# First modulation in four parts, and a last MLP group that gates W2 and adds onto x in the bank

## The chip, the cores and the metric

The kernel runs on one core of a Trainium2 chip. The metric is device microseconds of one execution. Engines are TensorE (PE; its weight loads are listed as PEld), VectorE (DVE), ScalarE (ACT), GpSimd (POOL) and SyncE (SP), which issues the transfers. All five run beside each other, each in the order of its own instruction stream, and wait for one another by semaphores.

## The reference, cut to what matters

Two layers work on 640 tokens, five tiles of 128 (tile 0 is context, tiles 1 to 4 are latents), with D_MODEL = 1024 and D_FF = 4096. Each sub-layer is

```
x <- LayerNorm(ALPHA * x + gate * f(x * (1 + scale) + shift)),   eps 1e-5
(shift, scale, gate) = columns of SiLU(cond) @ w_mod[l] + b_mod   (cond: c for latents, c_ctx for context)
layer 0: f = [retention | differential attention] @ w_out,  heads from one product with w_in
layer 1: f = [windowed attention | gated linear attention] @ w_out
MLP:     f(h) = square(relu(h @ w_1)) @ w_2
lambda of the differential attention = exp(sum(p0*p1)) - exp(sum(p2*p3)) + lam_init
```

Outputs are x of both groups, and keys, values and states of the context. The first step of all is shift and scale of layer 0, on which everything else depends; the last is the sum over D_FF in W2, the gate, the addition to x and a LayerNorm with its own g and b.

## The kernel before, in words

Every fp32 operand of a product is split into a high and a low part (fp32r), and a product becomes three: hi x hi, hi x lo, lo x hi. A weight comes in units of 128x1024 (512 KB): SP loads it into one of NRAW = 3 buffers `wraw`, ACT casts it to `whi`, and DVE subtracts to get `wlo` (`Unit.split`, line 525). A raw buffer is free again when `wlo` is made. Activations are kept in the same way (`h0h`, `h0l`; `ghi`, `glo` in the MLP).

The order of all instructions on PE, ACT, DVE and POOL is written into the program: a planner (`Order`) lets generators of work take turns by a time that it keeps for each engine, and what it has issued stays in that order. SP's order comes from the framework's scheduler; at most eight transfers are in flight, since each waits for the one eight before it. In the start, up to `start.close()`, the order is the one in which the code stands.

**The start** (lines 1000 to 1128) computes shift and scale of layer 0 in two halves of four feature tiles each. `load_mod0(h, k)` loads two tiles 128x512 of weights, `matvec` multiplies them by the SiLU of the conditioning vectors into a bank `mod0` (profile name `mod`; 32x256 products at line 468), `mod_row` copies it (ACT, `mrow`), `mod_cols` transposes it on PE (`modT`, line 483) and adds the bias on DVE (`first_mod`, `sc`), and `modulated` applies it to one token tile (ACT and POOL, `h`; then DVE's `h0h`, `h0l`). `early_part(t, h)` are the first products of layer 0's input projection for that half, into banks `early`; tiles 2 and 3 share a double bank. EARLY gives the step k of the second half's `matvec` ahead of which a tile's products stand; TURN is the order of tiles for the last half. `lam(dls)` computes the lambda above from `diff_lam`, whose load (`dl`) is issued after the first half's `xT` tiles.

**The end** is group g = 7 of eight in the last layer's MLP. Each group adds four blocks of 128 rows of W2. For the earlier groups the product is collected in `y`; in the last one, for each tile t and each half of the columns, `mlp_block` (line 1994) runs 12 products into a bank `fps`, DVE multiplies it by the gate row (`tmp`) and adds it to x. Then `norm` (line 929) takes statistics on DVE (`bn`, `mv`, `r`, `nmr`), ACT normalises, and POOL multiplies by g and adds b (`lnrow`), both 128x512; the last tile does all but its first quarter on DVE. SP sends x out in 11 transfers.

Line 379 is the helper through which all instructions of ACT, DVE and POOL go, 468 is a product, 483 a transpose, 452 a transfer. In the profile the digits of names are left out: `wmod` is also `w_mod0`'s tile, `sc` is `sc1`, `h` is `h32`.

Of the kernel before, what the change touches and what calls it, by code (L numbers as in the profile page):

```python
# [406 lines left out]
def trunk_kernel(ctx: ExitStack, tc: tile.TileContext, io: dict, layers: int = 2, stop: str = ""):  # L407
# [105 lines left out]
    class Unit:  # L513


        def __init__(self, src, kt, n, own=False):
            self.src, self.kt, self.n, self.own = src, kt, n, own
# [143 lines left out]
    done = set()  # L661
    pieces = {}
# [19 lines left out]
    for l in range(layers):  # L682
# [246 lines left out]
    def norm(t, rows, ft, A, B, final, key, xd=None):  # L929
# [4 lines left out]
        for i, (a, c0, c1) in enumerate(cuts):  # L934
            dve.bn_stats(st[:, i, :], X[t][a][:, c0:c1])
# [14 lines left out]
        if final:  # L950

            cut = (1024, 1024, 1024, 1024, 256)[t]
            for a, c0, c1 in ((0, 0, 256), (0, 256, 512), (1, 0, 512)) if t == NT - 1 else ((0, 0, 512), (1, 0, 512)):
                c, far = slice(c0, c1), 512 * a + c1 <= cut
                x, g, b = X[t][a][:, c], rows[0][a][:, c], rows[1][a][:, c]
# [7 lines left out]
                load(io["y"][t * P:(t + 1) * P, 512 * a + c.start:512 * a + c.stop], x)  # L963
            return
# [35 lines left out]
    def load_mod0(h, k):  # L1000
        raws[h, k] = [slot("wmod0"), slot("wmod0")]
        for a in range(2):
            load(raws[h, k][a][:, :512], io["w_mod0"][h, k, :, 512 * a:512 * a + 512])

    def matvec(h, k, ps):
        raw = raws.pop((h, k))
        for j in range(4):
            mm(ps[32 * j:32 * j + 32, :256], cs[:, k, :], raw[j // 2][:, 256 * (j % 2):256 * (j % 2) + 256],
               start=(k == 0), stop=(k == KT - 1))

    def load_x(h):
        xt = [slot("xT") for _ in range(4)]
        for k in range(4):
            load(xt[k][:, :TOK], io["xT"][4 * h + k])
        return xt

    def mod_row(ps):
        row = slot("mrow")
        act.copy(row[:, :256], ps[:, :256])
        return row  # L1020

    def mod_cols(h, row):
        tp = acc("modT")
        for e in range(2):
            transpose(tp[:, tcol(e)], row[:, tcol(e)])
        for s in range(2):
            o = V_BM + 8 * s + 4 * h
            vec_tt(first_mod[:, s, 4 * h:4 * h + 4, :].rearrange("p (b e) r -> p e b r", e=2),
                   tp[:, :256].rearrange("p (e s b r) -> p e s b r", e=2, s=2, b=2)[:, :, s, :, 0:2],
                   vec[:, o:o + 4].rearrange("p (b e) -> p e b", e=2).unsqueeze(3).broadcast_to([P, 2, 2, 2]), op=ALU.add)  # L1030
        dve.tensor_scalar(sc1[:, 4 * h:4 * h + 4, :], first_mod[:, 1, 4 * h:4 * h + 4, :], 1.0, None, op0=ALU.add)

    def modulated(h, xt, t):
        r_ = 1 if t == 0 else 0
        h32 = slot("h32")
        for b in range(4):
            k = 4 * h + b
# [5 lines left out]
        h4 = h32[:, :512].rearrange("p (b c) -> p b c", b=4)  # L1043
        hi = ft.h[h][:, :, tcol(t)]
        dve.tensor_copy(hi, h4)
        vec_tt(ft.l[h][:, :, tcol(t)], h4, hi.bitcast(F32), op=ALU.subtract)
# [7 lines left out]
    def early_part(t, h):  # L1054
        for n in range(2):
            w, o, c = pieces[0, EVEN[n]], early_bank(t)[:, 256 * n:256 * n + 256], tcol(t)
            for k in range(4 * h, 4 * h + 4):
# [9 lines left out]
    def lam(dls):  # L1067
# [16 lines left out]
    load_unit()  # L1084
    xt = load_x(0)
    load_unit()
    load_unit()
    ps = acc("mod0")
    for k in range(KT):
        matvec(0, k, ps)  # L1090
    row = mod_row(ps)
    split_unit()
    load_unit()
# [3 lines left out]
    for k in range(KT):  # L1097
        load_mod0(1, k)
    xt1 = load_x(1)
    load(cst[:, C_RC:], io["consts"][:, C_RC:])  # L1100
    mod_cols(0, row)
    order.give()
    warm(early_bank(0)[:, :128], 14)
    modulated(0, xt, 0)
    split_unit()
    for t in range(1, NT):
        modulated(0, xt, t)
    split_unit()
    split_unit()
    lam(dls)  # L1110
    ps = acc("mod0")
    for k in range(KT):
        for t in range(NT):
            if EARLY[t] == k:
                early_part(t, 0)
        matvec(1, k, ps)
    row = mod_row(ps)
    early_part(3, 0)
    mod_cols(1, row)
    order.give()  # L1120
    early_part(4, 0)
    load_unit()
    for t in TURN:
        modulated(1, xt1, t)
# [162 lines left out]
    def even_mixer(ft, cat, out_half):  # L1287
# [221 lines left out]
        for t in TURN:  # L1509
            split_hold[0] = t in TURN[:2]  # L1510

            def step():
                pos[1] = 2
                early_part(t, 1)
# [411 lines left out]
    def layer(l, ft, xd):  # L1926
# [34 lines left out]
        for g in range(8):  # L1961
# [14 lines left out]
            else:  # L1976
                if g == 6:
                    need_mods(l, (5,))
                    rows = gate_rows(l, 1)
                for f in range(4):  # L1980
# [13 lines left out]
            def mlp_block(t, nh):  # L1994
                w = use((l, "2", g, nh), (l, "2", g, 0) if last else None)
# [149 lines left out]
```

## Time and profile before

| | |
|---|---|
| median of three runs | 1635.65 us (1634.84 to 1637.54) |
| the profiled execution | 1635.63 us, of it the span 1633.8 us |
| TensorE busy | 1570.0 us, 96% |
| DVE, ACT, POOL busy | 62%, 37%, 32% |
| mean granted TensorE clock | 0.993 |
| chain that ended last, by engine | PE 80%, DVE 6%, ACT 5%, POOL 4%, DMA 2% |
| transfers | 177.75 MB, 109 GB/s over the span |

An engine's busy time is a sum over the whole span. The change is at its two ends, so the lines to read are those of the first 65 us and of the last 45 us. A line of a timeline gives start, duration, engine, program line, operation, result and operand, and in brackets how long the engine was idle before it and what it waited for; like instructions that follow each other are put together (x4), and their duration is then that of the whole stretch.

### The profile page before, as it was taken

Reading aid. Unit: us, or ns where it says so; the run is one execution under the profiler, and the core shown is the slowest. Engines: PE = TensorE matmul, PEld = TensorE weight load, DVE = VectorE, ACT = ScalarE, POOL = GpSimd, SP = SyncE. Lnnn points to the kernel's source line nnn. Section 1 sums busy time; section 2 is a strip of 40 time slices with the busy share of each in tenths; the row PEclk is TensorE's granted clock in tenths of the full one; section 3 lists DMA queues with packets and bytes.
Section 4 is the critical chain, followed back from the end, with each engine's and each line's share of the span. In section 5 each row is a group of like instructions: output and inputs, shape, how many; then the busy total and the mean of one; then the engine's idle time right before and its main releaser. Section 6 shows DMA issues by size and latency. Waiting matters only on the chain.

```text
span 1633.8 us, 28517 instructions
## 1 busy us (share of the span) xinstructions
PE 1570.0 (96%) x11345; PEld 1421.7 (87%) x11345; DVE 1018.0 (62%) x1943; ACT 610.4 (37%) x1279; POOL 524.7 (32%) x451
## 2 busy tenths in 40 slices
PE   7999999999999999999999998889999999999996
PEld 4998999999889889988988887779989988998994
DVE  3776662676477677676786788777824444444457
ACT  2554443336323222222255555553633222322321
POOL 2110000012467777777537347231200010011226
PEclk9999999999999999999999999999999999999998
DMA  9633334341444444463324101114212222223121
GB/s 333 204 119 118 102 98 162 130 134 52 139 136 143 148 139 152 147 182 114 112 68 139 61 28 39 56 43 155 79 52 78 78 78 72 71 75 113 58 78 65
DMA packets 89844, 177.75 MB, mean 109 GB/s; under 512 B 23648, under 2 KB 30832, under 8 KB 89712
## 3 DMA queue, kind: packets, MB, share of 16 engines
q1 hardware_dynamic: 89712, 175.94, 33.6%
q8 instruction: 89, 1.46, 0.4%
q14 instruction: 43, 0.35, 0.1%
HBM read 169.40 MB, written 6.50 MB: 108 GB/s over the span
## 4 chain that ended last, share of the span: by engine, by line
PE 80%; DVE 6%; ACT 5%; POOL 4%; DMA 2%; issue 2%; SPq 0%; POOLq 0%; DVEq 0%; ACTq 0%
PE ff L468 25%; PE fps L468 24%; PE proj L468 11%; PE ops L468 6%; PE fproj L468 3%; ACT h L379 1%; PE early L468 1%; DMA wmod<-in_w_mod 1%; POOL x L379 1%; PE sd L468 1%; PE po L468 1%; DVE wlo L379 1%; POOL y L379 1%; PE odp L468 1%; PE gl L468 1%
## 5 line engine op out<-in xcount | busy, mean ns | idle before, releaser
L468 PE MATMUL ff<-hh,whi 128*128 128x320 f32 (+2 forms) x960 | 297.2, 310 | 0.0
L468 PE MATMUL ff<-hh,wlo 128*128 128x320 f32 (+2 forms) x960 | 296.5, 309 | 0.1
L468 PE MATMUL ff<-hl,whi 128*128 128x320 f32 (+2 forms) x960 | 296.4, 309 | 0.0
L379 ACT CAST whi<-wraw 128x1024 fp32r<-128x1024 f32 (+1 forms) x183 | 189.3, 1045 | 285.4 <-PE fps L468 250.5
L379 DVE TENSOR_TENSOR wlo<-wraw,whi 128x1024 fp32r<-128x1024 f32 (+1 forms) x183 | 244.2, 1339 | 68.8 <-ACT whi L379 68.6
L468 PE MATMUL fps<-wlo,ghi 128*128 128x512 f32 (+1 forms) x648 | 253.9, 392 | 2.0 <-DVE wlo L379 2.0
L468 PE MATMUL fps<-whi,ghi 128*128 128x512 f32 (+1 forms) x648 | 254.5, 393 | 0.0
L468 PE MATMUL fps<-whi,glo 128*128 128x512 f32 (+1 forms) x648 | 253.5, 391 | 0.0
L379 POOL TENSOR_TENSOR x<-x,lnrow 128x512 f32<-128x512 f32 (+1 forms) x78 | 110.4, 1429 | 347.9 <-DVE y L379 216.7
L468 PEld LDWEIGHTS ff<-hh,whi 128*128 128x128 f32 x960 | 180.2, 188 | 3.1 <-issue 2.1
L379 DVE TENSOR_TENSOR relu<-relu 128x320 f32<-128x320 f32 (+3 forms) x100 | 64.1, 641 | 189.5 <-ACT ghi L379 185.9
L468 PEld LDWEIGHTS ff<-hl,whi 128*128 128x128 f32 x960 | 180.2, 188 | 0.6
L468 PEld LDWEIGHTS ff<-hh,wlo 128*128 128x128 f32 x960 | 180.2, 188 | 0.4 <-DVE wlo L379 0.4
L379 ACT ACTIVATE relu<-ff 128x320 f32<-128x320 f32 (+3 forms) x100 | 51.4, 514 | 295.2 <-PE ff L468 295.2
L379 DVE TENSOR_TENSOR y<-fps,y 128x512 f32<-128x512 f32 x120 | 82.6, 689 | 117.8 <-PE fps L468 117.7
L468 PEld LDWEIGHTS fps<-wlo,ghi 128*128 128x128 f32 x648 | 121.8, 188 | 29.9 <-DVE wlo L379 2.9
L468 PEld LDWEIGHTS fps<-whi,ghi 128*128 128x128 f32 x648 | 121.6, 188 | 29.6 <-issue 2.5
L468 PEld LDWEIGHTS fps<-whi,glo 128*128 128x128 f32 x648 | 121.7, 188 | 28.0
L379 POOL TENSOR_SCALAR wmod<-wmod,cs 128x512 f32<-128x512 f32 x84 | 95.2, 1134 | 124.1 <-DVE moda L379 108.5
L379 POOL TENSOR_TENSOR moda<-moda,wmod 128x512 f32<-128x512 f32 x84 | 123.5, 1470 | 6.2
L468 PE MATMUL ops<-wlo,cath 128*128 128x256 f32 x320 | 90.2, 282 | 2.2 <-DVE wlo L379 2.2
L468 PE MATMUL proj<-whi,hh 128*128 128x256 f32 (+1 forms) x280 | 83.9, 300 | 8.6 <-DVE sg L379 5.7
(295 smaller groups left out, 3372.2 us busy)
## 6 DMA issues: line engine op xcount, KB each, us to landing
wraw<-in_w SPq DMA_DIRECT2D x128, 512.0 KB
wmod<-in_w_mod SPq DMA_DIRECT2D x128, 256.0 KB
wmodp<-in_w_mod SPq DMA_DIRECT2D x64, 256.0 KB
wraw<-in_w_even SPq DMA_DIRECT2D x24, 512.0 KB
wraw<-in_w_out SPq DMA_DIRECT2D x16, 512.0 KB
wraw<-in_w_odd SPq DMA_DIRECT2D x16, 512.0 KB
gate<-mrow SPq DMA_DIRECT2D x16, 256.0 KB
xT<-in_xT SPq DMA_DIRECT2D x8, 320.0 KB
```

Source lines behind the costliest of these rows:

```text
L379: i = f(*a, **k)
L468: nc.tensor.matmul(o, a, b, **kw)
```

## The change

1. The first modulation is done in four quarters of two feature tiles: `w_mod0` comes as [4, 8, 128, 512], one transfer for each step k, `matvec` has 32x128 products, `load_x` loads two tiles at a time, `modulated` does two feature tiles. The start is one loop over the quarters. In it the load of `dl`, with those of `sink` and the constants, stands behind the last quarter's `xT`, and `lam(dls)` stands in the second quarter's turn.
2. For the latent tiles the last group's four units of W2 are loaded once more as `("gated", n)`; POOL multiplies them by the gate's columns before they are split. Tile 0 uses the ungated units.
3. For the latent tiles ACT copies x into the bank (tile `out`) behind a dummy product that starts the bank; the block's products add onto it. DVE's product with the gate and its addition to x are gone; `norm` reads the banks.
4. In the final `norm` the second half of tiles 1 to 3 goes to DVE, in two passes, where it was on ACT and POOL; the last tile has four parts of 256 columns, and there are 12 output transfers.

```diff
@@ Unit.split
+            if self.gate is not None:
+                for k in range(self.kt):
+                    c = slice(k * self.n, (k + 1) * self.n)
+                    pool.tensor_tensor(raw[:, c], raw[:, c], last_gates[self.gate][:, :self.n], op=ALU.mult)
@@ order of the weights, behind the last layer's pieces
+    for n in range(2):
+        add_piece(("gated", n), [Unit(io["w_2"][layers - 1, 7, n, u], 2, 512, gate=n) for u in range(2)])
@@ norm: source() gives the bank where there is one, else X[t][a]
-            dve.bn_stats(st[:, i, :], X[t][a][:, c0:c1])
+            dve.bn_stats(st[:, i, :], source(a, c0, c1))
...
-            cut = (1024, 1024, 1024, 1024, 256)[t]
+            cut = (1024, 512, 512, 512, 256)[t]
...
                 if far:
-                    act.activation(x, x, AF.Identity, scale=r, bias=nmr)
+                    act.activation(x, y, AF.Identity, scale=r, bias=nmr)
...
                 else:
-                    stt(x, x, mv[:, 0:1], g, op0=ALU.subtract, op1=ALU.mult)
+                    stt(x, y, mv[:, 0:1], g, op0=ALU.subtract, op1=ALU.mult)
@@ start
+    for q in range(3):
+        for k in range(KT):
+            load_mod0(q, k)
+        if q == 0:
+            load_unit()
+        xts.append(load_x(q))
...
     for k in range(KT):
-        load_mod0(0, k)
...
+        load_mod0(3, k)
+    xts.append(load_x(3))
     dls = slot("dl")
     bc_row(dls[:, :256], io["diff_lam"])
     bc_row(sk, io["swa_sink"])
-    for k in range(KT):
-        load_mod0(1, k)
-    xt1 = load_x(1)
     load(cst[:, C_RC:], io["consts"][:, C_RC:])
...
+    for q in range(4):
         for t in range(NT):
+            if q or t:
+                modulated(q, xts[q], TURN[t] if q == 3 else t)
+        if q == 3:
+            break
+        if q == 1:
+            split_unit()
+            split_unit()
+            load_unit()
+            lam(dls)
+        ps = acc("mod0")
+        for k in range(KT):
+            for t in range(NT):
+                if EARLY[t] == k:
+                    early_part(t, q)
+            matvec(q + 1, k, ps)
+        row = mod_row(ps)
+        early_part(3, q)
+        mod_cols(q + 1, row)
+        order.give()
+        early_part(4, q)
@@ last group of the last layer
+                def preload():
+                    if todo:
+                        t, a, c0, c1 = todo.pop(0)
+                        ps = (acc if t in (1, 3) or c0 else pss)("out", True)
+                        banks.setdefault(t, {})[a, c0, c1] = ps
+
+                        hv = parts[0][0]
+                        mm(ps[:, :c1 - c0], hv[:, :128], hv[:, :c1 - c0], start=True, stop=False)
+                        act.copy(ps[:, :c1 - c0], X[t][a][:, c0:c1])
+
+                def whole_block(t, a, c0, c1):
+                    preload()
+                    w = use(("gated", a), ("gated", 0))
+                    c, n, ps = tcol(t), slice(c0, c1), banks[t][a, c0, c1][:, :c1 - c0]
+                    for f in range(4):
+                        hv, lv = parts[f]
+                        mm(ps, hv[:, c], w.hi(f, n), start=False, stop=False)
+                        mm(ps, hv[:, c], w.lo(f, n), start=False, stop=False)
+                        mm(ps, lv[:, c], w.hi(f, n), start=False, stop=(f == 3))
...
+                        for b in blocks:
+                            if b[0] == t:
+                                order.gemm(lambda: whole_block(*b))
```

**Where the instructions stand.** SP's order in the start, in before: the load of `dl` (`diff_lam`) stands ahead of the second half's weights `wmod0`.

```order
L452 DMA rd_522<-in_ret_decay 128x8
L452 DMA wmod_967_5452<-in_w_mod 128x512
L452 DMA wmod_968_5454<-in_w_mod 128x512
L452 DMA dl_36_202<-in_diff_lam 128x256
L452 DMA wmod0_37_205<-in_w_mod0 128x512
L452 DMA wmod0_38_206<-in_w_mod0 128x512
```

SP's order in the changed kernel, where the load of `dl` is row 53:

```order
L452 DMA wmod0_56_262<-in_w_mod0 128x512
L452 DMA wmod0_57_264<-in_w_mod0 128x512
L452 DMA xT_58_266<-in_xT 128x640
L452 DMA xT_59_267<-in_xT 128x640
L452 DMA dl_60_270<-in_diff_lam 128x256
L452 DMA wraw_77_427<-in_w_even 128x1024
```

The load moved behind all 32 tiles `wmod0` and all eight `xT`. DVE's order in the changed kernel around the use of `dl`; `first_mod` here is that of the third quarter:

```order
L379 TENSOR_TENSOR wlo_76_424<-wraw_39_228,whi_75_423 128x1024
L379 TENSOR_TENSOR dl_60_270<-dl_60_270 128x128
L379 TENSOR_REDUCE ls_109<-dl_60_270 128x2
L379 TENSOR_TENSOR nlam_110<-ls_109 128x1
L379 TENSOR_SCALAR nlam_110<-nlam_110 128x1
L379 TENSOR_SCALAR nsink_112<-sink_111 128x8
L379 TENSOR_TENSOR first_mod_100<-modT_80_518,vec_87 128x4 x2
L379 TENSOR_SCALAR sc1_101<-first_mod_100 128x4
L379 CAST h0h_2_103<-h32_81_535 128x2x128
```

In before the same rows stand in the same order, with the second half's `first_mod` behind them. POOL's order at the end of the program in before; `y` belongs to the groups ahead, `x` to the final products of tiles 0 and 1:

```order
L379 TENSOR_TENSOR y_2376_14079<-y_2376_14079,gate_2667_16313 128x512
L379 TENSOR_TENSOR x_2162_12786<-x_2162_12786,lnrow_2746_17011 128x512
L379 TENSOR_TENSOR x_2201_13014<-x_2201_13014,lnrow_2747_17013 128x512
L379 TENSOR_TENSOR x_2162_12786<-x_2162_12786,lnrow_2748_17015 128x512
L379 TENSOR_TENSOR x_2201_13014<-x_2201_13014,lnrow_2749_17017 128x512
L379 TENSOR_TENSOR x_2168_12831<-x_2168_12831,lnrow_2746_17011 128x512
```

The same place in the changed kernel; `wraw` are the four units of W2 that POOL gates, each in two halves:

```order
L379 TENSOR_TENSOR y_2392_14187<-y_2392_14187,gate_2683_16421 128x512
L379 TENSOR_TENSOR wraw_2758_17059<-wraw_2758_17059,gate_2682_16419 128x512 x2
L379 TENSOR_TENSOR wraw_2761_17091<-wraw_2761_17091,gate_2682_16419 128x512 x2
L379 TENSOR_TENSOR wraw_2787_17186<-wraw_2787_17186,gate_2683_16421 128x512 x2
L379 TENSOR_TENSOR x_2178_12894<-x_2178_12894,lnrow_2764_17123 128x512
L379 TENSOR_TENSOR x_2217_13122<-x_2217_13122,lnrow_2765_17125 128x512
L379 TENSOR_TENSOR x_2178_12894<-x_2178_12894,lnrow_2766_17127 128x512
L379 TENSOR_TENSOR x_2217_13122<-x_2217_13122,lnrow_2767_17129 128x512
L379 TENSOR_TENSOR wraw_2800_17239<-wraw_2800_17239,gate_2683_16421 128x512 x2
L379 TENSOR_TENSOR x_2184_12939<-x_2184_12939,lnrow_2764_17123 128x512
```

Three units stand ahead of tile 0's four final products, the fourth behind them. ACT's order at that place in the changed kernel; `whi` are the casts of the units, `out` the copies of x into banks, `x` the final activations of tile 0:

```order
L379 CAST whi_2780_17157<-wraw_2748_16960 128x1024
L379 COPY out_2782_17161<-x_2184_12939 128x512
L379 COPY out_2788_17188<-x_2222_13156 128x512
L379 CAST whi_2785_17182<-wraw_2758_17059 128x1024
L379 CAST whi_2789_17193<-wraw_2761_17091 128x1024
L379 COPY out_2801_17241<-x_2194_12987 128x512
L379 ACTIVATE sq_2794_17215<-mv_2792_17210,eps_t_90 128x1
L379 ACTIVATE x_2178_12894<-x_2178_12894,nmr_2797_17218,r_2796_17217 128x512
L379 ACTIVATE x_2217_13122<-x_2217_13122,nmr_2797_17218,r_2796_17217 128x512
L379 CAST whi_2798_17235<-wraw_2787_17186 128x1024
L379 CAST whi_2802_17246<-wraw_2800_17239 128x1024
```

The casts of the gated units come behind copies of x, and those of the third and fourth unit behind the final activations of tile 0.

## Rows read from the trace of the kernel before

**Rows 1.** Page, part 1: busy us, share, instructions.

```profile
PE 1570.0 (96%) x11345; PEld 1421.7 (87%) x11345; DVE 1018.0 (62%) x1943; ACT 610.4 (37%) x1279; POOL 524.7 (32%) x451
```

**Rows 2.** Chain of waits, first 62 us: start us, duration us, what.

```profile
36.62 0.62 PE mod L468 x4
...
44.78 0.22 PE modT L483 x2
44.99 17.09 PE early L468 x144
```

**Rows 3.** Windows: us, busy PE PEld DVE ACT POOL, PE clock, DMA share, GB/s.

```profile
0.00:9.00 9.00, 2.63 (x12) 0.59 (x12) 0.92 (x6) 1.50 (x2) 0.20 (x4) 1.00 0.75 230
9.00:18.00 9.00, 8.29 (x52) 2.09 (x52) 0.00 (x0) 0.17 (x1) 0.00 (x0) 1.00 0.97 336
18.00:27.00 9.00, 7.17 (x54) 6.40 (x54) 5.48 (x11) 6.04 (x13) 5.56 (x7) 1.00 1.04 392
27.00:36.00 9.00, 7.10 (x59) 4.08 (x60) 5.07 (x7) 2.21 (x3) 2.53 (x4) 1.00 0.97 340
36.00:47.00 11.00, 10.95 (x101) 9.16 (x102) 1.94 (x10) 2.06 (x6) 1.36 (x3) 1.00 1.04 400
```

**Rows 4.** Timeline of DVE, ACT and POOL, 36 to 53 us.

```profile
36.14 0.28 DVE L379 TENSOR_TENSOR dl<-dl 128x128 f32<-128x128 f32 x1
36.46 0.29 DVE L379 TENSOR_REDUCE ls<-dl 128x2 f32<-128x128 f32 x1
...
36.78 0.20 ACT L379 ACTIVATE ls<-ls 128x2 f32<-128x2 f32 x1 [1.81 <-DVE ls L379]
41.79 0.37 ACT L379 COPY mrow<-mod 128x256 f32<-128x256 f32 x1 [4.80 <-PE mod L468]
...
45.03 0.24 DVE L379 TENSOR_TENSOR first_mod<-modT,vec 128x8 f32<-128x8 f32 x2 [7.59 <-PE modT L483]
...
45.64 7.14 POOL L379 TENSOR_SCALAR h<-xT,sc,first_mod 128x128 f32<-128x128 f32 x10 [16.11 <-DVE sc L379]
...
46.56 0.43 DVE L379 CAST h0h<-h 128x512 fp32r<-128x512 f32 x1 [1.08 <-POOL h L379]
```

**Rows 5.** Timeline of PE: a later modulation's 32x128 products.

```profile
64.86 1.08 PE L468 MATMUL modp<-wmodp,cs 128*32 128x128 f32 x32
```

**Rows 6.** Windows around a gap of TensorE, columns as in Rows 3.

```profile
1056.00:1058.00 2.00, 0.00 (x0) 0.00 (x0) 1.76 (x10) 1.91 (x6) 0.00 (x0) 0.66 0.76 279
1058.00:1060.00 2.00, 0.73 (x3) 0.76 (x4) 1.36 (x7) 1.64 (x6) 1.22 (x2) 0.50 0.01 2
1060.00:1062.00 2.00, 2.00 (x12) 2.00 (x11) 0.00 (x0) 2.00 (x7) 1.65 (x2) 0.50 0.00 0
1062.00:1064.00 2.00, 2.00 (x13) 2.00 (x12) 0.48 (x2) 1.07 (x3) 1.63 (x3) 0.63 0.00 0
```

**Rows 7.** Chain of waits, last 49 us: the last group's first products.

```profile
1589.73 2.81 PE fps L468 x12
```

**Rows 8.** Timelines of ACT, DVE, POOL and PE, last 46 us.

```profile
1590.67 1.04 ACT L379 CAST whi<-wraw 128x1024 fp32r<-128x1024 f32 x1
...
1593.90 1.22 DVE L379 TENSOR_TENSOR wlo<-wraw,whi 128x1024 fp32r<-128x1024 f32 x1
...
1604.95 0.69 DVE L379 TENSOR_TENSOR tmp<-fps,gate 128x512 f32<-128x512 f32 x1
...
1621.13 0.41 DVE L379 BATCH_NORM_STATS2 bn<-x 128x6 f32<-128x256 f32 x1
...
1622.98 0.74 DVE L379 SCALAR_TENSOR_TENSOR x<-x,mv,lnrow 128x256 f32<-128x256 f32 x1
...
1605.21 5.97 POOL L379 TENSOR_TENSOR x<-x,lnrow 128x512 f32<-128x512 f32 x4 [38.45 <-ACT x L379]
1611.63 19.43 POOL L379 TENSOR_TENSOR x<-x,lnrow 128x512 f32<-128x512 f32 x14 [0.46 <-ACT x L379]
...
1618.55 0.28 PE L468 MATMUL fps<-whi,glo 128*128 128x256 f32 x1
```

More of the change, by code (lines that the diff above doesn't have):

```diff
@@ L513, in trunk_kernel, with __init__ @@
     class Unit:
-        def __init__(self, src, kt, n, own=False):
-            self.src, self.kt, self.n, self.own = src, kt, n, own
+        def __init__(self, src, kt, n, own=False, gate=None):
+            self.src, self.kt, self.n, self.own, self.gate = src, kt, n, own, gate
         def load(self):
@@ L927, in summed, with norm, source @@
             stt(x, x, ALPHA, y, op0=ALU.mult, op1=ALU.add)
-    def norm(t, rows, ft, A, B, final, key, xd=None):
+    def norm(t, rows, ft, A, B, final, key, xd=None, banks=None):
+        def source(a, c0, c1):
+            for (h, b0, b1), ps in (banks or {}).items():
+                if h == a and b0 <= c0 and c1 <= b1:
+                    return ps[:, c0 - b0:c1 - b0]
+            return X[t][a][:, c0:c1]
         cuts = [(0, 0, 512), (1, 0, 512)] if t < NT - 1 else [(0, 0, 256), (0, 256, 512), (1, 0, 256), (1, 256, 512)]
@@ L998, in trunk_kernel, with load_mod0, matvec, load_x @@
     raws = {}
[L1000 to L1006, printed above, removed]
-        for j in range(4):
[L1008 to L1014, printed above, removed]
+    def load_mod0(q, k):
+        raws[q, k] = slot("wmod0")
+        load(raws[q, k][:, :512], io["w_mod0"][q, k])
+    def matvec(q, k, ps):
+        raw = raws.pop((q, k))
+        for j in range(4):
+            mm(ps[32 * j:32 * j + 32, :128], cs[:, k, :], raw[:, tcol(j)], start=(k == 0), stop=(k == KT - 1))
+    def load_x(q):
+        xt = [slot("xT") for _ in range(2)]
+        for k in range(2):
+            load(xt[k][:, :TOK], io["xT"][2 * q + k])
         return xt
@@ L1018, in mod_row, with mod_cols, modulated @@
         row = slot("mrow")
-        act.copy(row[:, :256], ps[:, :256])
+        act.copy(row[:, :128], ps[:, :128])
         return row
-    def mod_cols(h, row):
+    def mod_cols(q, row):
         tp = acc("modT")
-        for e in range(2):
-            transpose(tp[:, tcol(e)], row[:, tcol(e)])
+        transpose(tp[:, :128], row[:, :128])
         for s in range(2):
[L1027 to L1033, printed above, removed]
+            o = V_BM + 8 * s + 2 * q
+            vec_tt(first_mod[:, s, 2 * q:2 * q + 2, :],
+                   tp[:, :128].rearrange("p (s b r) -> p s b r", s=2, b=2)[:, s, :, 0:2],
+                   vec[:, o:o + 2].unsqueeze(2).broadcast_to([P, 2, 2]), op=ALU.add)
+        dve.tensor_scalar(sc1[:, 2 * q:2 * q + 2, :], first_mod[:, 1, 2 * q:2 * q + 2, :], 1.0, None, op0=ALU.add)
+    def modulated(q, xt, t):
         r_ = 1 if t == 0 else 0
         h32 = slot("h32")
-        for b in range(4):
-            k = 4 * h + b
+        for b in range(2):
+            k = 2 * q + b
             scale, bias = sc1[:, k, r_:r_ + 1], first_mod[:, 0, k, r_:r_ + 1]
@@ L1979, in layer @@
                     rows = gate_rows(l, 1)
+                    if last_layer:
+                        last_gates.extend(rows[0])
                 for f in range(4):
@@ L1994, in mlp_block @@
             def mlp_block(t, nh):
-                w = use((l, "2", g, nh), (l, "2", g, 0) if last else None)
+                w = use((l, "2", g, nh), (l, "2", g, 0) if last and not last_layer else None)
                 c = tcol(t)
@@ L2071, in _layout @@
     wm = np.asarray(i["w_mod"])
[L2073 removed]
+    a["w_mod0"] = wm[0, :, :2048].reshape(8, 128, 2, 4, 256).transpose(3, 0, 1, 2, 4).reshape(4, 8, 128, 512)
     a["w_mod"] = wm.reshape(2, 8, 128, 12, 512).transpose(0, 3, 1, 2, 4)
```

90 lines of the change are left out of this document (44 added, 46 removed).

## Prediction

> **What bounds the kernel now.** I read the busy table first: TensorE works for 96% of the span and the next engine for 62% [rows 1], so the time falls only where TensorE waits or where the span runs on before its first or behind its last product. Both ends of the program are changed, so the views after that are of the ends: the chain of waits and the windows up to 60 us, then the chain and the timeline of the last 45 us.
>
> At the start the chain goes from the loads of the first modulation's weights to a product `mod` at 36.62, and from 41.7 on TensorE has no gap: 144 `early` products in 17.09 us, 0.119 us each, the last at 62.08 [rows 2]. The reader is to see that up to 36 us the transfers set the pace: 230, 336, 392 and 340 GB/s in four windows of 9 us, 400 behind them [rows 3]. At the end TensorE starts the last group's second products at 1589.73, which I call T0, and ends at T0+29.1 (1618.55 and 0.28) [rows 7, 8]. POOL, which multiplies and shifts the normalised tiles, ends at 1611.63 + 19.43 = 1631.06, T0+41.3 [rows 8]; the 2.7 us from there to the span's end are the last transfer. So POOL's backlog of 12.2 us behind TensorE is what the tail of the change could take away.
>
> The profiled execution took 1635.63 us, its span 1633.8, with 1.8 around it; the median of the runs is 1635.65. The sum is made on 1635.63.
>
> **The start.** The matrix-vector work keeps its bytes; it is issued as 32 loads as before. What matters is the load of `dl`: before, it stands ahead of the second half's weights; now it is SP's row 53, behind all 32 weight tiles and all eight of xT. Adding the sizes in SP's order up to it: 8,192 KiB of weights, 2,560 of xT, 2,048 of four `wraw`, 768 of three later modulation tiles, 675 of small ones including `dl`: 14,243 KiB or 14.58 MB. The windows' rates times 9 us give 2.07 + 3.02 + 3.53 + 3.06 = 11.68 MB by 36 us; the other 2.90 MB at 400 GB/s take 7.3, so `dl` has crossed at 43.3 [rows 3]. The before kernel gives the lag: its 11.44 MB up to the tile of the product at 36.62 cross at 35.3 by the same sum, so 1.3 us go by until use [rows 2]; `dl` is usable at 44.5.
>
> DVE and ACT run in order. `dl`'s product and sum on DVE and the exponential on ACT, which in before ran at 36.14 to 36.98 without a wait [rows 4], now stand ahead of the third quarter's `first_mod` (DVE) and `mrow` (ACT). Queued behind them is every step of that quarter and of the fourth, and the last casts of weights; TensorE runs dry at 38 to 39, when the products of the first two quarters are done. From 44.5: `dl` 0.28, sum 0.29, exponential 0.20, `mrow` up to 0.37, transpose 0.22, `first_mod` 0.24, scale about 0.17 (between its neighbours), `h` 0.71 (7.14 over 10), `h0h` up to 0.43 [rows 2, 4]: 2.9, and about 0.03 for each of nine hand-overs: 47.7 for the third quarter's first product. The fourth tile's leftover (12 products, 1.4) fits between. Then 60 products at 0.119 (7.1), eight steps of the matrix-vector work at 1.08 over 4 or 0.27 each (2.1) [rows 5], one transpose 0.2: 57.1. The fourth quarter's `first_mod` and `h` need the 2.0 that follow the transpose, and only 1.4 of products cover them: +0.5. Then 60 more products, 7.1, and one more wait: a tile's bank is shared by t=2 and t=3, and t=3 has to wait until the rotary products on DVE, which stand behind a `wlo` of 1.22, have read t=2; before, 24 products lay between, now 12 (1.4). I take 1.6 with the ends 0 and 2.6 (two `wlo` and a copy, less the cover). End 66.3 against 62.08: **+4.2**; ends +2 (`dl` overtakes half of the queue's 2.9 MB) and +8 (every transfer at the 340 of the fourth window, and the longer wait).
>
> TensorE is idle for some 6 to 7 us there, which before it never was. The nearest row: a gap around 1056 to 1059 has the granted clock at 0.66, then 0.50, then 0.63, and back at 1.00 in the window from 1064, so the lower level, 1.2 GHz. TensorE works in it for 0.73 + 2.00 + about 1.5 us (the part of the last 2 us that makes a mean of 0.63), 4.2 us at half rate [rows 6]: 2.1 us lost. In the start half of the work after the gap waits for `h` anyway: **+1.0**, ends 0 and 2.1.
>
> The order of layer 0's mixer (60 to 320 us) moves by a few places on all engines, with the same instructions. I take **0**, ends -3 and +4, about the size of the waits met at the start.
>
> **The tail.** Gone are, for the latent tiles, eight products with the gate and eight additions on DVE (0.69 a piece [rows 8]); DVE waits there, so their removal is worth only what the last tile's chain holds of them. Added are nine dummy products of up to 512 columns (0.234 each, 2.81 over 12 [rows 7]): 2.1 us on TensorE; and, on POOL, eight products of 128x512 that gate four units of W2. POOL's rate is 1.39 to 1.49 a product (19.43 over 14, 5.97 over 4 [rows 8]), so 2.8 to 3.0 a unit.
>
> The place that decides is the fourth gated unit. Three units stand on POOL ahead of the four final products of tile 0, the fourth behind them. In before POOL starts those four at 1605.21 and ends them at 1611.18 (T0+21.45); they wait for tile 0's statistics, which the change does not bring earlier (tile 0 keeps its old path). Then the fourth unit's gating, 2.8: T0+24.2; its cast on ACT 1.04, 25.3; its `wlo` on DVE 1.22, 26.5 [rows 8]; the last products of tile 1's second block 1.2: T0+27.7. TensorE by then has done tile 0's two blocks and tile 1's first, due at about T0+12.5, and waits: the casts of the first gated units also stand behind a copy of x into the bank, and the third unit's cast behind both final activations of tile 0. What remains is five blocks of 12 products and a dummy, 13 x 0.234 = 3.0 each, 15.1, and the last block in halves of 24 x 0.119 with its dummies, 3.1: T0+45.9 against T0+29.1, +16.8.
>
> Behind TensorE less is left than the 12.2 of before. For the last tile: statistics 0.41, six one-column instructions at 0.2 (the size of `ls`, [rows 4]) 1.2, six passes of 256 columns on DVE at 0.41 to 0.74 [rows 8], 2.5 to 4.4; up to 1.5 of tile 3 still ahead. Together 4.1 to 7.5; I take 5.8. The end is T0+51.7 against T0+41.3: **+10.4**; ends +7 (POOL at its faster rate and the cast started on the unit's first half) and +13 (7.5 behind TensorE, and 1 more where passes on DVE beside POOL go at the 0.74).
>
> TensorE has two waits of 4 to 5 us in that stretch. Rows 6 are the nearest again: **+1.5**, ends 0 and 2.1. The Trainium skill ("TensorE: Matmul & The Clock Gate", section "HAM oscillation — how this bites in real kernels") says that a kernel whose products are shorter than its waits for data starts each block cold, and pays for it every time. Before agrees in one place (0.50 behind the gap at 1056); its gaps are too few to show the repetition. By that rule the sum is the 17.1 below; without it, 14.6.
>
> Sum: 4.2 + 1.0 + 0 + 10.4 + 1.5 = 17.1 us, 1635.6 + 17.1 = **1652.7**.
>
> **The rivals.**
> 1. *The tail is late, the start is not.* For it: 128 KB is a small transfer, and its descriptors may finish ahead of the large ones. Against it: in [rows 2] a tile's use follows the sum of bytes by 1.3 us. 1635.6 + 11.9 = 1647.5.
> 2. *The start is late, the tail gains.* The fourth unit's gating would have to be done before T0+12.5. For it: its load can begin when a third raw buffer falls free. Against it: POOL's order, in which nothing passes. The tail without stalls: 29.1 + 2.1 + 5.8 = T0+37.0, -4.3. With +5.2 at the start: 1636.5.
> 3. *Faster: both ends as the change has them on paper.* The mechanism is one: TensorE gets its data before it runs dry, at the start since a quarter's `h` is ready earlier than a half's, at the tail since x in the bank takes DVE's passes away behind the last product. The price is -4.3 for the tail and some -2 at the start (of the 5.2 us between 36.62 and 41.79 that are spent on the last half). It decides if `dl` lands before 38 and the fourth unit is split by T0+12.5. For it: POOL and DVE are far from full [rows 1]. Against it: both orders. 1629.3.
>
> **How the numbers follow.** Forecast (both ends late) 0.86, its own range 1645 to 1662; rival 1 0.06; rival 2 0.03; rival 3 0.05. The terms' ends add up to +6 and +29; not all fall on one side, so 8 in 10 lies in 1644 to 1663, which takes rival 1 in. A measurement of this kernel can tell 0.2% (3.3 us) from no change. Faster by more than that: rival 3, 0.05. Within it: rival 2, 0.03. Slower: the forecast and rival 1, 0.92.
>
> **What would show it.** In the profile after: DVE's product of `dl` at 44 to 45, with a wait of some 8 us before it; TensorE idle from about 38 to 45; the last `early` product near 66; a granted clock below 1 behind both gaps. In the tail: the waits of `whi` on ACT for POOL's `wraw`, POOL's fourth gating at T0+21 to 24, TensorE's end near T0+46 and 6 us from there to the last instruction. It is wrong if `dl` runs before 38, or if POOL gates all four units ahead of tile 0's final products.

## The result, and the profile after

| | before | changed |
|---|---|---|
| median | 1636.6 us (4 runs) | 1657.5 us (4 runs) |
| ratio | 1 | 1.0128, 95% interval 1.0111 to 1.0146 |
| profiled execution | 1635.63 us, span 1633.8 | 1656.55 us, span 1654.4 |
| last `early` product ends | 62.1 | 67.4 |
| first product of layer 0's output projection (`ops`) | 313.9 | 323.9 |
| T0, the last group's first product with W2 | 1589.7 | 1597.8 |
| TensorE's end, behind T0 | +29.1 | +48.9 |
| last instruction of DVE, ACT or POOL, behind T0 | +41.3 | +53.7 |

The change costs 21 us, against 17.1 forecast. The span's 20.6 divide into 5.3 at the start, 2.8 between the start and T0 (4.6 at first, of which 1.8 are regained) and 12.4 behind T0. These are one execution of each kernel; how far such numbers move between executions of the same instructions is told under plan_shift.

**The start.** The chain of waits of the changed kernel, 0 to 80 us (start, duration, what), answers to [rows 2]:

```profile
37.88 6.11 DMA dl<-in_diff_lam
44.01 0.30 DVE dl L379
44.34 0.30 DVE ls L379
44.66 0.04 ACT ls L379
...
44.78 0.24 ACT mrow L379
...
45.07 0.33 PE modT L483
```

The load of `dl` is now a link of it, and behind it come, one after the other, the instructions that stood at 36.14 to 36.98 beside other work [rows 4]. The timelines of DVE and PE show who waited:

```profile
44.01 0.29 DVE L379 TENSOR_TENSOR dl<-dl 128x128 f32<-128x128 f32 x1 [5.95 <-DMA dl<-in_diff_lam]
...
45.07 0.33 PE L483 MATMUL modT<-cst,mrow 128*128 128x128 f32 x1 [3.56 <-ACT mrow L379]
...
64.27 0.39 PE L468 MATMUL early<-whi,h0h 128*128 128x256 f32 x1 [1.15 <-ACT v L379]
```

The 3.56 us are the wait behind `dl`; the 1.15 us are the double bank of tiles 2 and 3. The windows (columns as in [rows 3]) show the clock behind the first:

```profile
40.00:42.00 2.00, 1.51 (x12) 1.31 (x12) 0.00 (x0) 0.00 (x0) 0.00 (x0) 1.00 1.07 381
42.00:44.00 2.00, 0.00 (x0) 0.00 (x0) 0.00 (x0) 0.00 (x0) 0.00 (x0) 1.00 1.01 391
44.00:46.00 2.00, 0.93 (x8) 0.93 (x9) 1.37 (x8) 0.46 (x3) 0.00 (x0) 1.00 0.91 363
46.00:48.00 2.00, 2.00 (x11) 2.00 (x11) 1.36 (x4) 1.94 (x5) 1.97 (x4) 0.50 0.14 45
48.00:50.00 2.00, 2.00 (x22) 1.86 (x24) 1.90 (x7) 0.00 (x0) 1.25 (x2) 0.65 0.00 0
```

All engines stand still from 42 to 44 while the transfers run at 391 GB/s; then TensorE works 2.0 and about 1.4 us at half rate, 1.7 us lost.

Another wait stands earlier: up to 22.34 TensorE is idle for 4.04 us for a tile `wmod` of weights, with the clock at 0.53 and 0.62 from 22 to 26, where before has waits of 1.09 and 1.59 us (22.91, 28.62) and a clock of 1.00.

**The middle.** In layer 0's mixer TensorE waits for `qkh` longer than in before, where the longest such wait behind the start is 1.28 us, with the lower clock behind it (timeline and windows of the changed kernel):

```profile
159.77 0.63 PE L468 MATMUL sd<-qkh,qkh 128*128 128x320 f32 x1 [3.21 <-DVE qkh L379]
```

```profile
160.00:162.00 2.00, 2.00 (x10) 1.96 (x10) 1.19 (x2) 0.44 (x1) 0.00 (x0) 0.50 0.00 0
162.00:164.00 2.00, 2.00 (x10) 2.00 (x9) 0.84 (x3) 1.53 (x4) 0.00 (x0) 0.50 0.00 0
164.00:166.00 2.00, 2.00 (x11) 2.00 (x10) 1.97 (x4) 0.89 (x2) 0.00 (x0) 0.63 0.00 0
```

**The tail.** POOL's timeline, against its two rows in [rows 8]:

```profile
1606.67 4.49 POOL L379 TENSOR_TENSOR wraw<-wraw,gate 128x512 f32<-128x512 f32 x2 [9.29 <-DMA wraw<-in_w]
1614.51 5.94 POOL L379 TENSOR_TENSOR x<-x,lnrow 128x512 f32<-128x512 f32 x4 [3.35 <-ACT x L379]
1620.41 2.48 POOL L379 TENSOR_TENSOR wraw<-wraw,gate 128x512 f32<-128x512 f32 x2
```

The fourth unit is gated behind tile 0's four products, without any wait between. ACT and TensorE wait for it:

```profile
1622.92 1.04 ACT L379 CAST whi<-wraw 128x1024 fp32r<-128x1024 f32 x1 [6.85 <-POOL wraw L379]
...
1616.12 0.79 PE L468 MATMUL out<-whi,ghi 128*128 128x512 f32 x1 [4.39 <-ACT whi L379]
1618.14 0.80 PE L468 MATMUL out<-wlo,ghi 128*128 128x512 f32 x1 [1.22 <-DVE wlo L379]
1624.02 0.80 PE L468 MATMUL out<-whi,ghi 128*128 128x512 f32 x1 [3.38 <-ACT whi L379]
1625.28 0.79 PE L468 MATMUL out<-wlo,ghi 128*128 128x512 f32 x1 [0.47 <-DVE wlo L379]
```

Products of 512 columns read 0.39 us at full rate (0.49 or 0.50 for the first behind a wait) and 0.63 to 0.80 here; the windows have the clock at 0.52, 0.50, 0.50 and 0.78 in four stretches of 4 us from 1616:

```profile
1616.00:1620.00 4.00, 2.66 (x5) 1.78 (x6) 1.98 (x1) 0.07 (x1) 4.00 (x3) 0.52 0.00 0
1620.00:1624.00 4.00, 0.64 (x2) 0.00 (x0) 0.00 (x1) 1.04 (x1) 2.89 (x3) 0.50 0.35 131
1624.00:1628.00 4.00, 3.52 (x7) 2.44 (x8) 2.02 (x3) 0.00 (x0) 0.00 (x0) 0.50 0.01 4
1628.00:1632.00 4.00, 4.00 (x15) 3.20 (x14) 3.14 (x10) 1.62 (x3) 0.57 (x1) 0.78 0.00 1
```

### The profile page after: what moved, and what is told of

Its sections match the earlier page's. It is cut to its first block, busy times and chain, and to the rows that moved or that the text cites. A ratio compares the mean times of both kernels' runs of the same rounds, so it can differ in the third digit from the quotient of the medians.

```text
span 1654.4 us, 28880 instructions
## 1 busy us (share of the span) xinstructions
PE 1580.8 (96%) x11482; PEld 1435.7 (87%) x11482; DVE 1025.3 (62%) x1963; ACT 617.0 (37%) x1291; POOL 525.5 (32%) x453
## 4 chain that ended last, share of the span: by engine, by line
PE 83%; DVE 6%; ACT 4%; DMA 3%; issue 2%; POOL 1%; SPq 0%; POOLq 0%; ACTq 0%; DVEq 0%
PE ff L468 26%; PE fps L468 25%; PE proj L468 11%; PE ops L468 6%; PE fproj L468 3%; DMA wmod<-in_w_mod 2%; ACT h L379 1%; PE out L468 1%; PE sd L468 1%; PE odp L468 1%; PE po L468 1%; PE early L468 1%; DVE wlo L379 1%; PE gl L468 1%; PE ss L468 1%
## 5 line engine op out<-in xcount | busy, mean ns | idle before, releaser
L379 ACT CAST whi<-wraw 128x1024 fp32r<-128x1024 f32 (+1 forms) x187 | 193.3, 1045 | 283.1 <-PE fps L468 247.8
L379 DVE TENSOR_TENSOR wlo<-wraw,whi 128x1024 fp32r<-128x1024 f32 (+1 forms) x187 | 249.8, 1341 | 71.8 <-ACT whi L379 71.5
L468 PE MATMUL fps<-wlo,ghi 128*128 128x512 f32 (+1 forms) x612 | 240.1, 392 | 1.8 <-DVE wlo L379 1.8
L468 PE MATMUL fps<-whi,ghi 128*128 128x512 f32 (+1 forms) x612 | 240.9, 394 | 0.0
L468 PE MATMUL fps<-whi,glo 128*128 128x512 f32 (+1 forms) x612 | 240.3, 393 | 0.0
L379 POOL TENSOR_TENSOR x<-x,lnrow 128x512 f32<-128x512 f32 (+1 forms) x72 | 100.4, 1402 | 329.9 <-DVE y L379 215.8
L468 PEld LDWEIGHTS fps<-wlo,ghi 128*128 128x128 f32 x612 | 115.0, 188 | 28.3 <-DVE wlo L379 2.7
L468 PEld LDWEIGHTS fps<-whi,ghi 128*128 128x128 f32 x612 | 114.9, 188 | 27.8 <-issue 2.5
L468 PEld LDWEIGHTS fps<-whi,glo 128*128 128x128 f32 x612 | 114.9, 188 | 26.5
## 6 DMA issues: line engine op xcount, KB each, us to landing
wmod<-in_w_mod SPq DMA_DIRECT2D x128, 256.0 KB
wmodp<-in_w_mod SPq DMA_DIRECT2D x64, 256.0 KB
gate<-mrow SPq DMA_DIRECT2D x16, 256.0 KB
```

Source lines behind the costliest of these rows:

```text
L379: i = f(*a, **k)
L468: nc.tensor.matmul(o, a, b, **kw)
```

## The experiments

Ratios are to the kernel before on the same chip, with 95% intervals. The columns "early", "ops", T0 and the two ends behind T0 are read from each run's trace as in the table above; between kernels with the same instructions up to T0 (the changed one, `norm0_late`, `norm0_again`, `t0_dve`, `no_gate`) T0 alone differs by 2.6 us, so single differences below that say little.

| run | ratio | early | ops | T0 | PE end | last |
|---|---|---|---|---|---|---|
| before | 1 | 62.1 | 313.9 | 1589.7 | +29.1 | +41.3 |
| changed | 1.0128 (1.0111 to 1.0146) | 67.4 | 323.9 | 1597.8 | +48.9 | +53.7 |
| start_only | 1.0053 (1.0039 to 1.0066) | 67.2 | 322.4 | 1595.1 | +29.3 | +41.7 |
| tail_only | 1.0082 (1.0068 to 1.0096) | 60.4 | 315.3 | 1591.8 | +48.9 | +53.7 |
| dl_early | 1.0123 (1.0109 to 1.0138) | 63.1 | 320.1 | 1598.1 | +48.9 | +53.7 |
| t0_dve | 1.0092 (1.0076 to 1.0107) | 65.8 | 321.0 | 1595.3 | +43.2 | +48.0 |
| norm0_late | 1.0071 (1.0058 to 1.0083) | 67.4 | 323.8 | 1597.9 | +38.4 | +43.2 |
| no_gate | 1.0052 (1.0038 to 1.0065) | 66.0 | 321.4 | 1595.6 | +35.1 | +39.9 |
| plan_shift | 1.0033 (1.0022 to 1.0043) | 61.5 | 317.8 | 1595.0 | +29.2 | +41.4 |
| tail_late_raw4 | 1.0018 (1.0008 to 1.0029) | 60.9 | 312.8 | 1588.5 | +38.8 | +43.6 |
| tail_casts_raw4 | 0.9990 (0.9981 to 1.0000) | 60.6 | 312.5 | 1589.6 | +34.8 | +39.5 |
| before_raw4 | 0.9996 (0.9987 to 1.0005) | 61.2 | 314.5 | 1589.0 | +29.1 | +41.3 |
| dl_norm0 | 1.0072 (1.0057 to 1.0086) | 64.3 | 319.8 | 1597.2 | +38.4 | +43.1 |
| norm0_again | 1.0070 (1.0058 to 1.0082) | 65.9 | 322.9 | 1598.0 | +40.0 | +44.7 |

**start_only**: the hunks of the start and of `w_mod0`'s layout alone. 

> The start in four quarters as in the changed kernel, the end as before. My theory: the two ends are independent, and the start costs what the profile of the changed kernel shows up to the last group's first product (1597.82 against 1589.73, +8.1 us): about 1644.5 us. Rival: most of the 4.6 us that arise between 67 and 324 us are an accident of that run or tied to the end's planning, then about 1640 us.

**tail_only**: the other hunks alone. 

> The start as before, the end with gated units and x in the bank. My theory: the tail alone costs its +12.4 us (last instruction 53.7 us behind the last group's first product against 41.3): about 1649 us. Rival: the tail is late only because the start is late (its loads come later): then it would be at or below 1640 us.

0.53% and 0.82% make 1.35%, against 1.28% for both: within the intervals the two ends add up, so neither needs the other. Both rivals fall; the tail is late with an early start too.

**dl_early**, the start's suspected cause taken away:

```diff
@@ first quarter, behind load_x(0) and the second unit
+            dls = slot("dl")
+            bc_row(dls[:, :256], io["diff_lam"])
+            bc_row(sk, io["swa_sink"])
@@ behind load_x(3)
-    dls = slot("dl")
-    bc_row(dls[:, :256], io["diff_lam"])
-    bc_row(sk, io["swa_sink"])
```

> The changed kernel, with the loads of dl and sink issued behind the first quarter's xT and second unit; the order of all instructions on PE, DVE, ACT and POOL is that of the changed kernel, only SP's differs. My theory for the start: lam's wait for dl held DVE and ACT, so DVE's product of dl is done before 38 us, TensorE is not idle for more than 3 us there, the last early product is back at 62 to 63 us (67.1 now), 5 us gained. For the mixer behind it, theory A: its +4.6 us come from the new order of its instructions and stay (about 1652 us in all). Theory B: they come from transfers that start late because the start is late, and go (about 1648 us). Rival for the start: the bytes alone hold it, dl is no longer last but the third quarter's weights are as late: under 2 us gained.

DVE's timeline:

```profile
38.30 0.28 DVE L379 TENSOR_TENSOR dl<-dl 128x128 f32<-128x128 f32 x1
```

There is no wait, and the last `early` product comes 4.3 us sooner: the place was right, and the rival of the bytes falls. It is still 1.0 us later than in before: the wait for `wmod` at 22 us is here too (4.43 us), and it is no effect of `dl`. The stretch of the mixer stays long (257.0 us from early to ops, 256.5 in the changed kernel, 251.8 in before), so it does not come from transfers that start late: theory B of the mixer falls. But T0 is no earlier, and the whole is not measurably faster, where both theories expected 5 us or more. The gain goes in the middle: by DVE's instructions, which can be matched one to one, the lead of dl_early is 5.3 us at 207, 3.8 from 220 to 500, 2.9 at 800, 1.4 at 818 and gone at 918. Two of these steps have a row. At 805 TensorE waits 1.33 us for a `wlo` that takes 2.33 beside POOL. And at 910 the clock falls in dl_early (first row) and not in the changed kernel (second), in a stretch without any wait:

```profile
910.00:912.00 2.00, 2.00 (x33) 1.88 (x24) 1.05 (x4) 1.99 (x4) 2.00 (x4) 0.53 0.00 0
```

```profile
910.00:912.00 2.00, 2.00 (x44) 1.43 (x43) 1.83 (x5) 1.97 (x3) 2.00 (x4) 1.00 0.03 8
```

**dl_norm0** (norm0_late, below, with dl_early's edit) and **norm0_again** (norm0_late once more) ask whether that was one execution's chance. 

> norm0_late with the early loads of dl and sink of dl_early (only SP's order differs from norm0_late). In dl_early the last early product came 4.3 us sooner and the whole was no faster. Theory A: the loss behind it (between 164 and 913 us, where nothing of the change stands) was one execution's: which stretches fall to the lower clock and how DVE and POOL meet; then this one is 3 to 5 us faster than norm0_again, which runs beside it: about 1.0045 times before. Theory B: work in the middle is held by something that does not move with the start, and takes the gain back every time: within 1 us of norm0_again, 1.007 times before.

> norm0_late once more, on the same chip as dl_norm0, for the comparison with it: 1.0058 to 1.0083 times before. Its profile is a second one of the same instruction order, so the spread of the start of the last group (1595 to 1598 us in the five kernels with this start) can be read from one kernel.

Medians 1647.8 and 1647.7: no gain again, as theory B has it, with an interval that excludes more than some 3 us. Here the last `early` product is only 1.6 us sooner; dl_norm0 has a lower clock from 20 to 30 us (0.50 from 22 to 28), norm0_again only from 22 to 26. The stretch from the first W2 product of layer 0 to the first `gl` product takes 500.8 and 502.0 us with the early load and 497.8 to 499.4 in the six profiles with the late one. What takes the gain back in all is not settled, and theory B's cause, something that does not move with the start, was not found; the drop of the clock near 910 is in both early ones (and in before) and in none of the six late ones, and accounts for about 1.5 us.

**plan_shift**, the mixer's order by itself, in the kernel before:

```diff
     order.fifo = False
+    order.pass_to(order.now + 12.0)
     mod_left[0] = order.now
```

> The kernel before, with only the planner's own clock set 12 us later at the end of the start, as the changed start does to it (41.3 to 53.3 of the planner's units): the start's instructions are the same, and some 60 of TensorE's 9327 rows stand elsewhere in layer 0's mixer. Theory A (the mixer's +4.6 us come from the new order, a draw of the planner): the stretch from the last early product to the first ops product, 251.8 us in before and 256.5 in the changed kernel, changes by 2 us or more. Theory B: the order does not matter by itself, the stretch stays within 1 us of 251.8 and the time within 0.1% of before.

The start is before's; the first `ops` product stands at 317.77 against 313.93 in before, with the last `early` product 0.5 us sooner (timeline of TensorE):

```profile
317.77 0.39 PE L468 MATMUL ops<-whi,cath 128*128 128x256 f32 x1
```

256.2 us for the stretch instead of 251.8, and 0.33% on the whole. One window over this stretch (columns as in [rows 3]) divides it into busy and idle time of TensorE; the rows are before, plan_shift, the changed kernel and tail_only:

```profile
62.08:313.93 251.85, 244.55 (x2382) 232.23 (x2380) 156.82 (x478) 111.71 (x305) 8.05 (x5) 1.00 0.40 125
61.54:317.77 256.23, 247.01 (x2380) 234.02 (x2380) 157.61 (x478) 111.75 (x305) 8.06 (x5) 0.99 0.38 122
67.38:323.86 256.48, 247.50 (x2381) 235.56 (x2379) 159.32 (x482) 112.12 (x307) 7.18 (x5) 0.99 0.40 126
60.41:315.29 254.88, 247.60 (x2381) 235.43 (x2379) 157.06 (x478) 111.59 (x305) 8.06 (x5) 0.99 0.39 123
```

TensorE is idle for 7.3 us in before, 9.2 in plan_shift and 9.0 in the changed kernel. The five profiles with before's order (before, tail_only, tail_late_raw4, tail_casts_raw4, before_raw4) all have 7.3 and the eight with the changed order 8.9 to 9.0, so 1.7 of the 4.6 us are waits that come with the order. The other 2.9 are busy time. That is not the order's: tail_only has before's order and the changed kernel's busy time, with a clock of 0.83 at 150 to 160 and at 200 to 210 us, where before has 1.00. So theory A holds for the waits (1.9 us in plan_shift), and the rest of the 4.6 comes from setting the changed kernel beside a profile of before without any lower clock in this stretch. Over all profiles of these two orders the stretch takes 251.8 to 254.9 us with before's order (mean 252.8) and 255.2 to 257.0 with the changed one (mean 256.0).

**t0_dve**: `cut = (0, 512, 512, 512, 256)[t]`, tile 0's final norm on DVE. 

> The changed kernel, but the final norm of tile 0 is done by DVE in two passes for each half instead of by ACT and POOL; POOL then gates the fourth unit without four products ahead of it. Nothing else moves on any engine. My theory: the fourth unit's wlo is ready at about 1618 instead of 1625.2 us, the second wait of TensorE (3.4 us and its half-rate stretch) goes, 7 us gained: about 1650 us. Rival: the third and fourth unit are held by the three raw buffers and their loads, so the wait only changes its name: gain under 2 us. Another: DVE's four passes, in front of the third unit's wlo, take the place of POOL's: gain about 3 us.

PE's timeline:

```profile
1611.10 0.50 PE L468 MATMUL out<-whi,ghi 128*128 128x512 f32 x1 [1.84 <-ACT whi L379]
1615.35 0.79 PE L468 MATMUL out<-wlo,ghi 128*128 128x512 f32 x1 [3.75 <-DVE wlo L379]
```

TensorE no longer waits for POOL's fourth gating behind tile 0's products, and 5.7 us are gained behind T0, between the theory's 7 and the second rival's 3. DVE's passes take part of it, as that rival said: the longer wait now names DVE's `wlo`.

**norm0_late**, the order of POOL, ACT and DVE mended:

```diff
+                    if last_layer and t == 0:
+                        continue
+                    if last_layer and t == 1:
+                        order.spawn(norm(0, ln, ft_n, A, B, True, ("h", l, 0), xd[0]))
                     order.spawn(norm(t, ln, ft_n, A, B, last_layer, ("h", l, t), xd[t], banks.get(t)))
```

> The changed kernel, but tile 0's final norm is issued behind tile 1's blocks: on POOL all four units are gated ahead of tile 0's final products, on ACT their casts stand ahead of its activations, on DVE their wlo ahead of its statistics. PE and SP keep their order. My theory (POOL's, ACT's and DVE's order held the fourth unit): its wlo is ready some 18 us behind the last group's first product instead of 27.5, TensorE ends at +40 to +41 instead of +48.9, the last instruction is at +45 to +46 instead of +53.7: 8 us gained, about 1649 us. Rival: raw buffers and loads held it all along, then the fourth unit is ready at +23 or later, and under 4 us are gained.

PE's timeline:

```profile
1613.43 0.49 PE L468 MATMUL out<-whi,ghi 128*128 128x512 f32 x1 [1.65 <-ACT whi L379]
1614.80 0.50 PE L468 MATMUL out<-wlo,ghi 128*128 128x512 f32 x1 [0.88 <-DVE wlo L379]
```

The fourth unit's first product is at T0+15.6 instead of +26.2, and the two products shown run at full rate. 10.5 us are gained behind T0, 2.5 more than expected. norm0_again, the same instructions once more, has the same two waits but a lower clock behind them, and gains 9.0:

```profile
1616.00:1620.00 4.00, 4.00 (x12) 3.12 (x11) 2.74 (x7) 0.61 (x2) 0.00 (x0) 0.57 0.01 4
```

The raw buffers are not what held the fourth unit.

**no_gate**: `gate=n` left out of the four units. 

> The changed kernel without the product of W2's four units with the gate (so that part of the computation is left out); units loaded again, x in the bank and all else stay. My theory: without POOL in the way the fourth unit hangs on its load alone (landed at about +13.3, cast and wlo by +16), TensorE ends at +38 to +39, 10 us gained. Rival: the cost sits in the copies of x into the bank and the dummy products rather than in gating, then under 5 us are gained.

 The last instruction is at +39.9, 13.8 us sooner than in the changed kernel (10 were expected) and 1.4 sooner than in before. Copies, dummy products and the second loads together cost less than the passes that they save; gating, with the order that it brings, is the whole price of the tail. The two cannot be told apart here: without gating the planner also puts the first unit's cast on ACT ahead of the copy of x into the second bank, and the casts of the third and fourth unit ahead of tile 0's final activations.

**tail_late_raw4**: before's start, norm0_late's tail, NRAW = 4. 

> The start as before; the end with gated units and x in the bank, tile 0's final norm behind tile 1's blocks, and four raw buffers instead of three (all engines but SP keep their order with that). My theory: with the fourth buffer the last unit's load starts before the first gated unit is split, and the waits shrink to about 3 us: TensorE ends at +34 to +36, the last instruction at +39 to +41 against +41.3 in before: 1632 to 1637 us, no change or 0.2% faster. Rival: casts and wlo of the four units, 2.3 us each one after the other behind TensorE's first blocks, are the next bound: +43 and more, slower than before by 2 us or more.

**before_raw4**: before with NRAW = 4. 

> The kernel before with four raw buffers instead of three and nothing else (all engines keep their order, only SP's differs). It is the control for the two runs with four buffers. My theory: no wait of before hangs on a raw buffer for more than a us in all, so within 0.15% of before. Rival: the stalls of TensorE in the mixers shrink, 2 us faster.

 No difference can be told, so the fourth buffer by itself helps or hurts nothing that shows.

tail_late_raw4 ends at +43.6 where +39 to +41 were expected, so its theory fails; the rival's +43 is met, though not by the casts and `wlo` that it named. Five waits of 0.76 to 1.65 us stayed. One is at the last ungated `wlo` (0.80; before has 1.02 there); four are behind copies of x into banks, which on ACT stand ahead of the gated casts and wait for a dummy product.

**tail_casts_raw4** mends that:

```diff
-                                if nh:
+                                if not nh:
                                     preload()
+                                elif last_layer:
+                                    use(("gated", 0), (l, "2", g, 1))
                                 mlp_block(t, nh)
```

In `whole_block`, `use` also stands ahead of `preload()`, and the planner takes gating at 0.2 us a product. 

> As tail_late_raw4 (start as before, tile 0's norm behind tile 1's blocks, four raw buffers), and the first two gated units are split during tile 0's second block, so that their casts on ACT and wlo on DVE stand ahead of the copy of x into the second bank and of DVE's work on tile 0's second half; the first bank's copy stands one block earlier. My theory: the four waits of 0.77 to 1.65 us in tile 1's first block and a half go, 3 us less, the last instruction at +39 to +40.5 behind the last group's first product against +41.3 in before and +43.6 in tail_late_raw4: 1633 to 1636 us, within 0.2% of before, on the fast side. Rival: the waits only collect at the fourth unit, whose load still starts when the last ungated unit is split: +42 or more, 0.1% slower than before.

```profile
1603.04 0.49 PE L468 MATMUL out<-whi,ghi 128*128 128x512 f32 x1 [0.79 <-ACT whi L379]
1604.30 0.50 PE L468 MATMUL out<-wlo,ghi 128*128 128x512 f32 x1 [0.77 <-DVE wlo L379]
```

These are the two waits at the fourth unit. Two more are left, 1.02 us at the last ungated `wlo` and 0.94 at the third unit's; the waits of 1.65 us are gone, and the last instruction is at +39.5. 0.9990 (0.9981 to 1.0000) is the lowest ratio of all versions, 1.4% below the changed kernel's and just at the edge of what can be told from before; against before_raw4 it is not told apart.

## Why the prediction was right, point by point

Both ends are late, as forecast, and the total is 20.9 us slower against 17.1. The tail went by the mechanism that was forecast, and runs show it. At the start the wait was there too, but that it makes the total longer is not shown, and the agreement is in part luck.

- *`dl` usable at 44.5, and DVE, ACT and TensorE in a row behind it*: 44.01, and they did wait in that row. TensorE ran dry at 41.5, not 38 to 39, so its gap was 3.56 us and not 6 to 7; the last `early` product's end, forecast at 66.3 and 1.0 more for the clock, was 67.4. The single terms differ more than their sum: the bank's wait was 1.15 us (1.6 forecast), the clock took 1.7 (1.0). That the sum met 67.4 so closely is in part luck. The six profiles with the late load have it at 65.8 to 67.4, since the gap is 1.9 to 3.6 us and the clock falls behind it in four of them. And with `dl` early it is at 63.1 and 64.3, against 60.4 to 62.1 in the six with before's start: about half of the lateness is not the wait for `dl`. The wait for `wmod` at 22 us, which is in all eight profiles with the new start, has no term in the sum.
- *That this lateness reaches the end in full*: assumed without a word in the sum, and not borne out. dl_early and dl_norm0 take 1.6 to 4.3 us of it away and gain nothing that can be measured. start_only shows that the new start costs 0.53%; which part of it does, stays open.
- *"The order of layer 0's mixer ... I take 0, ends -3 and +4"*: the term that was mis-sized most, and no row was given for its 0. In the recorded pair it measured +4.6 at the first `ops` product, outside its ends, and +2.8 at T0. Over all profiles of the two orders the stretch is 3.3 us longer, inside the ends: 1.7 are waits that the new order brings every time, the rest is busy time, which differs between executions with how often the clock falls.
- *The fourth gated unit*: forecast by its stations behind T0, `wlo` ready at +26.5; it was ready at 1625.23, +27.4. POOL's four products ended at +22.6 (21.45 forecast), the gating at +25.1 (24.2). norm0_late shows that this order was the cause: 9.0 to 10.5 of the tail's 12.4 us go with it.
- *TensorE's end at +45.9 and 1.5 for the clock*: +48.9. The four windows from 1616 lose 1.3, 0.3, 1.8 and 0.9 us to the clock, 4.3 in all, but not all of it reaches the end: the first two stand ahead of the fourth unit, which POOL holds whatever TensorE does. From the fourth unit's `wlo` to TensorE's end it was 21.5 us instead of 19.4, so 2.1 for the clock where 1.5 were forecast; the other 0.9 is the unit itself. Behind TensorE 4.8 us remained (5.8 forecast). The tail came to 12.4 against 11.9.
- *The rule of the Trainium skill* ("TensorE: Matmul & The Clock Gate", section "HAM oscillation — how this bites in real kernels") was worth 2.5 us of the sum. Rows now show its pattern: behind two waits, 4.39 and 3.38 us, the products start at the lower clock (0.52 and 0.50 in the windows). The measurement lies nearer to the sum with it, and beyond it; the clock took 1.7 us at the start and 2.1 at the end. At shorter waits it goes either way: behind the same 1.65 and 0.88 us the clock stays at 1.00 in norm0_late and falls to 0.57 in norm0_again.
- *The rivals.* Rival 3 (both ends faster) and rival 2 (the tail gains) fall with tail_only's 1.0082; rival 1 (start harmless) falls with start_only's 1.0053, though the wait for `dl` alone may be harmless to the total.

## What to carry to other kernels

A load that moves back in a queue has to be followed to its first reader, and from there along everything behind that reader in the order of its engine: 128 KB for a constant that is needed much later stopped DVE, ACT and TensorE for 2 us. Whether that reaches the end has to be tried: here taking the wait away gave nothing on the whole. Work put on an idle engine is late when it stands behind work of another tile, so the order to check is that of the engine that takes it over (9.0 to 10.5 us here, without one instruction more or less). And where a planner orders a long stretch, a change ahead of it shifts its order; allow for that as a term with ends of its own (0.33% from nothing but the planner's clock). To size it, set several profiles of each order beside each other: the waits came out alike in all, the busy time differed by 3 us between executions of one order.

## What the runs showed of the hardware

The granted clock also falls without a wait. In before, TensorE is busy for 2.00 of 2.00 us in each of these windows and the clock goes to 0.76, 0.50 and 0.89; ahead of the drop stand small products (`z`, 32x320, and `gd`, 64x64):

```profile
902.00:904.00 2.00, 2.00 (x45) 1.93 (x45) 1.54 (x4) 1.97 (x3) 2.00 (x4) 0.76 0.00 0
904.00:906.00 2.00, 2.00 (x11) 2.00 (x11) 1.39 (x3) 2.00 (x5) 1.15 (x2) 0.50 0.00 0
906.00:908.00 2.00, 2.00 (x17) 2.00 (x16) 1.96 (x4) 1.60 (x3) 0.00 (x0) 0.89 0.00 0
```

In the changed kernel the same products pass at 1.00. Even one order of instructions shows both: of the five profiles with before's order, before, tail_late_raw4 and tail_casts_raw4 have the drop, tail_only and before_raw4 do not. So two executions of the same instructions differ by one or two us at this place. The same holds behind a wait: after the gap at 45 us in the six profiles with the late `dl` the clock falls behind gaps of 3.56, 2.02, 1.87 and 1.99 us, and not behind 2.38 (t0_dve) and 2.99 (norm0_again).

DVE and POOL can slow each other. Of two `wlo` on DVE that ran beside POOL's gating from 1606.56, the first took 1.23 us and the second 2.31, where one in before takes 1.22 [rows 8]. POOL's two products there took 4.49 us together, where the two at 1620.41, with DVE idle, took 2.48.
